# Where the modulated input and three heads' value weights begin in SBUF, in a pooling and mLSTM layer

## The chip, the cores and the metric

One core of a Trainium2 chip runs the kernel, in one launch. The metric is the device time of one execution in microseconds (us); lower is better. Three runs of the kernel before gave 889.26, 889.43 and 889.63 us, so the median is 889.43 us.

## The reference

One layer of a latent-token backbone: 512 latent tokens and 256 context tokens, 1024 channels, everything in fp32. Cut to what matters here:

```
a_lat = rmsnorm(x)   * norm_mix * (1 + sc1)  + sh1        # 512 x 1024, the modulated input
a_ctx = rmsnorm(ctx) * norm_mix * (1 + csc1) + csh1       # 256 x 1024
p     = a @ w_in      # pooled input, q, k, v, o, two branch gates, 16 mLSTM gate columns
h     = bidirectional mLSTM(q, k, v, gates), 4 heads of 256, chunks of 128
y     = sigmoid(p[5]) * pool_mixer(p[0]) + sigmoid(p[6]) * readout(h, p[4])
x     = x + g1 * (y @ w_out)
x     = x + g2 * (silu(b @ w_g) * (b @ w_u)) @ w_ffn_out,   b = modulated rmsnorm(x)
out   = rmsnorm(x) * norm_final
```

Only the latent tokens are an output. The context tokens need keys, values and gates, but no queries.

## The kernel before, in words

**Layout.** Activations lie transposed: channels on the 128 partitions, tokens along the free axis. The modulated input is eight tiles of 128 channels by 512 latent tokens, and the context's eight tiles of 256 tokens two to a buffer. Precision comes from splitting: every fp32 operand x is held as a high part (x rounded to the type fp32r) and a low part (x minus the high part), and a product is three matmuls, high by high, high by low and low by high. So the latent modulated input takes 16 buffers of the tag `a`, and the context's 8: 24 buffers of 128 x 512 values, 2048 bytes on each partition.

**The stages, in order.** (1) `mod_rows`, `mod_cols` and `stage` (lines 261 to 329) make scale and shift, the tiles of `a` (`modulate`, line 284: ACT writes the high part, DVE the low) and six first output tiles at once (`products`, line 331, matmuls on line 334). (2) `values(0)`, then for each of the four heads gates, queries, keys, values, `attention` and the pooling branch. A tile of 128 output columns of `a @ w_in` is made by `lat_tile` (line 403): `wload` (line 148) brings 128 x 1024 weights by DMA into a raw buffer, ACT rounds them into a `wh` buffer and DVE subtracts into a `wl` buffer, and `mm3` (line 180) does 24 matmuls with the weights as the stationary operand, which is loaded into TensorE, and a tile of `a` as the moving operand, which streams through it. `keys` (line 421) does the same for the 256 context tokens as well. (3) the output projection (`proj_out`), (4) the feed-forward network, whose input products are Strassen products (`front` and `back`) over tiles of the tag `hp`, and its second product (`ffn_out`) over tiles of the tag `act`.

**The order of the work.** Stage 1 and a part of stage 4 are written out by hand for PE, ACT and DVE; elsewhere a planner orders the instructions. The `wh` and `wl` buffers are two each, `wr` (raw) three.

**`values(h)`** (line 549) turns the roles round: a 128 x 128 block of `a` is stationary, the value weights of a head are moving, 256 columns of them (272 for head 0, with the 16 gate columns). For each of six token blocks it does 24 matmuls (lines 565 to 567).

**Where tiles begin.** Only the position of a tile's first byte on its partition, counted from a multiple of 256 bytes, is at issue here, so the list says where each matmul operand begins:

```
LINE = 256
NEXT = 48
def S(tag, dtype=F32):
    return tl(tag, [P, T], dtype, BUFS[tag], LINE)
wh, wl = (tl(t, [P, WMAX], F32R, 2, LINE)[:, skip:skip + n] for t in ("wh", "wl"))
_, wh, wl = wload(src[:, i * 4 * n:(i + 1) * 4 * n], 4 * n, skip=min(NEXT, WMAX - 4 * n))
tl("q", [P, T + NEXT], F32R, BUFS["q"], LINE)[:, NEXT:]
hp = [tl("hp", [P, NEXT + 7 * D + 4], F32R, 2, LINE) for _ in range(2)]
```

`S` puts every tile on a multiple of 256 bytes: `a`, `act`, `kq`, `Sp`, `oh`, `ol`. The weights of `wload` lie on one too, unless `skip` moves them. The queries and the Strassen operands `hp` begin 48 values, 192 bytes, behind a multiple (one of the seven parts of `hp`, T3, 208 bytes behind). The value weights of heads 1, 2 and 3 begin 192 bytes behind; those of head 0 are 1088 values to a half and fill the buffer, so `skip` is 0, and their four slices of 272 columns begin 0, 64, 128 and 192 bytes behind. Slices of 128 or 256 columns are 512 or 1024 bytes and keep the position of their tile.

Of the kernel before, what the change touches and what calls it, by code (L numbers as in the profile page):

```python
# [10 lines left out]
F32 = mybir.dt.float32  # L11
# [6 lines left out]
P = 128  # L18
D = 1024
KT = D // P  # L20
T = 512
# [9 lines left out]

BUFS = {"a": 24, "tmp": 7, "kq": 7, "q": 4, "E": 6, "Sp": 10, "m": 7, "pm": 4, "act": 16, "x1": 8, "oh": 5, "ol": 5}
LINE = 256
NEXT = 48
WMAX = KT // 2 * (DH + NG)
PBW = 15 * 71
# [13 lines left out]
def layer_kernel(ctx: ExitStack, tc, xT, cT, w0, w1, wv0, wv, wada_a, wada_b, par, crow, bg, wpool,  # L50
# [3 lines left out]
    cnt = [0]  # L54
    pools, homes, stacks = {}, {}, {}

    def open_pool(name, tags, side="left"):
        st = ExitStack()
        p = st.enter_context(tc.tile_pool(name=name, bufs=1, side=side, reuse_waits="tile"))
        pools[name] = p  # L60
        for t in tags:
            homes[t] = p
        stacks[name] = st
# [4 lines left out]
    def tl(tag, shape, dtype=F32, bufs=1, align=None):  # L68
        cnt[0] += 1
        return homes[tag].tile(shape, dtype, name=f"{tag}_{cnt[0]}", tag=tag, bufs=bufs, align_bytes=align)  # L70

    def S(tag, dtype=F32):
        return tl(tag, [P, T], dtype, BUFS[tag], LINE)

    ps = ctx.enter_context(tc.tile_pool(name="ps", bufs=4, space=PSUM))
    dram = ctx.enter_context(tc.tile_pool(name="dram", bufs=1, space=DRAM))
# [1 line left out]
    def PS(tag="ps"):  # L78
        cnt[0] += 1
        return ps.tile([P, 512], F32, name=f"{tag}{cnt[0]}", tag=tag, bufs=4)  # L80

    open_pool("main", ("wr", "wh", "wl", "tmp", "small", "rc", "rc2"))
    open_pool("ap", ("a",), "right")
    open_pool("mix", ("m", "pm", "pa", "pb"), "right")
    open_pool("kqp", ("kq", "q"))
    open_pool("st", ("x", "cx", "ada", "row"))
# [58 lines left out]
    def wide(tag, bufs=2):  # L145
        return tl(tag, [P, D], F32R, bufs, LINE)

    def wload(src, n, dst=None, skip=0):

        raw = tl("wr", [P, WMAX], F32, 3)  # L150
        nc.sync.dma_start(raw[:, :n], src)
        if dst is None:
            wh, wl = (tl(t, [P, WMAX], F32R, 2, LINE)[:, skip:skip + n] for t in ("wh", "wl"))
            nc.scalar.copy(wh, raw[:, :n])  # L154
            V.tensor_sub(wl, raw[:, :n], wh.bitcast(F32))  # L155
            return [(wh[:, i * P:(i + 1) * P], wl[:, i * P:(i + 1) * P]) for i in range(n // P)], wh, wl
        if dst == "wide":
            h, l = (wide(t)[:, skip:skip + n] for t in ("gh", "gl"))
            split(raw[:, :n], h, l)
            return [(h[:, i * P:(i + 1) * P], l[:, i * P:(i + 1) * P]) for i in range(n // P)], None, None  # L160
        if isinstance(dst, str):
            dst = (dst, dst)
        parts = []
        for c in range(0, n, T):
            m = min(T, n - c)
            h, l = (S(t, F32R) for t in dst)
            nc.scalar.copy(h[:, :m], raw[:, c:c + m])
            V.tensor_sub(l[:, :m], raw[:, c:c + m], h[:, :m].bitcast(F32))
            parts += [(h[:, i * P:(i + 1) * P], l[:, i * P:(i + 1) * P]) for i in range(m // P)]
        return parts, None, None  # L170

    def split(src, h, l):
        nc.scalar.copy(h, src)
        V.tensor_sub(l, src, h.bitcast(F32))
        return h, l

    def tsplit(src, tag):
        return split(src, S(tag, F32R), S(tag, F32R))
# [6 lines left out]
            nc.tensor.matmul(dst, wh, al, start=False, stop=False, skip_group_check=on)  # L185
            nc.tensor.matmul(dst, wl, ah, start=False, stop=last and i == n - 1, skip_group_check=on)  # L186

    def vload(src, n, i):

        _, wh, wl = wload(src[:, i * 4 * n:(i + 1) * 4 * n], 4 * n, skip=min(NEXT, WMAX - 4 * n))  # L190
        return [(wh[:, c * n:(c + 1) * n], wl[:, c * n:(c + 1) * n]) for c in range(4)]

    class SumSq:
# [90 lines left out]
    def modulate(src, r, scale, shift, h, l, between=None):  # L284
# [7 lines left out]
        V.scalar_tensor_tensor(l, t1, shift, h.bitcast(F32), ALU.add, ALU.subtract)  # L292
        return h, l

    aT, acT = [], []
    acc0 = [PS("ps" if i < 2 else "pat") for i in range(len(FIRST) - 1)] + [wbank]
    cxt = [tl("cx", [P, T], F32, 4) for _ in range(4)]
# [23 lines left out]
    def stage(k, r):  # L321

        n = len(FIRST) * P
        raw, wh, wl = tl("wr", [P, WMAX], F32, 3), tl("wh", [P, WMAX], F32R, 2, LINE), tl("wl", [P, WMAX], F32R, 2, LINE)
        nc.sync.dma_start(raw[:, :n], w0[k])
# [40 lines left out]
    for k in range(KT):  # L366
# [18 lines left out]
        if k in (5, 6):  # L385
            ctx_quad(4 * (k - 5))
    manual.__exit__(None, None, None)
    wv_first += vload(wv0, DH + NG, 1)
    acc0 = dict(zip(FIRST, acc0))


    def conv_part(acc, n, j, dsts=None):

        y = S("tmp")
        nc.scalar.activation(y[:, :n], acc[:, :n], AF.Identity, bias=pcol(C_CB, j), scale=pcol(C_CW, 16 + j))
        V.scalar_tensor_tensor(y[:, 1:n], acc[:, 0:n - 1], pcol(C_CW, j), y[:, 1:n], ALU.mult, ALU.add)
        V.scalar_tensor_tensor(y[:, 0:n - 1], acc[:, 1:n], pcol(C_CW, 32 + j), y[:, 0:n - 1], ALU.mult, ALU.add)
        s = S("tmp")
        tanh_half(s[:, :n], y[:, :n])
        gated(y[:, :n], s[:, :n], y[:, :n])  # L400
        return split(y[:, :n], *dsts) if dsts else tsplit(y, "kq")

    def lat_tile(idx):

        if idx in acc0:
            return acc0[idx]
        acc = PS()
        mm3(acc, wload(w1[idx], D)[0], aT)
        return acc
# [7 lines left out]
    def queries(h):  # L417
        return [conv_part(lat_tile(Q0 + 2 * h + dk), T, 2 * h + dk,
                          [tl("q", [P, T + NEXT], F32R, BUFS["q"], LINE)[:, NEXT:] for _ in range(2)]) for dk in range(2)]

# [97 lines left out]
    def late_mod(n, behind):  # L518

        for i in itertools.islice(late, n):  # L520
            wa = tl("pb", [P, PBW], F32, 2)
            nc.sync.dma_start(wa[:, :D], wada_b[i])
            with tc.issue_after(behind.ins):
                V.scalar_tensor_tensor(wa[:, :D], wa[:, :D], 0.5, crow_s, ALU.mult, ALU.mult,
                                       accum_out=mods[:, i:i + 1])
# [12 lines left out]
    def atok(i):  # L538

        src = acT if i < 2 else aT  # L540
        i -= 0 if i < 2 else 2
        return [(h[:, i * P:(i + 1) * P], l[:, i * P:(i + 1) * P]) for h, l in src]
# [6 lines left out]
    def values(h, wp=None):  # L549
        n = DH + NG if h == 0 else DH  # L550
        if wp is None:
            wp = vload(wv[h - 1], n, 0) + vload(wv[h - 1], n, 1)
        vh = tl("vh", [P, NTOK, DH + 2], F32R)
        vl = tl("vl", [P, NTOK, DH + 2], F32R)
        nc.gpsimd.memset(vh[:, :, DH:DH + 1].bitcast(F32), 1.0)
        nc.gpsimd.memset(vh[:, :, DH + 1:DH + 2].bitcast(F32), 0.0)
        nc.gpsimd.memset(vl[:, :, DH:DH + 2].bitcast(F32), 0.0)
        accs = {}
        for i, half in ((2, 0), (3, 0), (4, 0), (2, 1), (3, 1), (4, 1), (5, 0), (5, 1), (0, 0), (0, 1), (1, 0), (1, 1)):
            if half == 0:  # L560
                accs[i] = PS()
            acc = accs[i]
            for kk in range(4 * half, 4 * half + 4):
                (wh, wl), (ah, al) = wp[kk], atok(i)[kk]
                nc.tensor.matmul(acc[:, :n], ah, wh, start=kk == 0, stop=False)  # L565
                nc.tensor.matmul(acc[:, :n], ah, wl, start=False, stop=False)  # L566
                nc.tensor.matmul(acc[:, :n], al, wh, start=False, stop=kk == KT - 1)  # L567
            if half == 0:
                continue
            if h == 0:  # L570
                gsrc = acc[:, DH:DH + NG].rearrange("p (d c h) -> p d c h", d=2, c=2)
                bsrc = bgt.rearrange("p (d c h) -> p d c h", d=2, c=2)
                for d, j in ((0, i), (1, 1 - i if i < 2 else 7 - i)):
                    V.tensor_add(gif[:, :, d, j, :], gsrc[:, d], bsrc[:, d])
            nc.scalar.copy(vh[:, i, :DH], acc[:, :DH])
            low = V.tensor_sub(vl[:, i, :DH], acc[:, :DH], vh[:, i, :DH].bitcast(F32))
            if h:
                late_mod(1, low)
        return vh, vl
# [266 lines left out]
    for h in range(H):  # L846
        tg = None
        if h == 0:
            mgate_all(0)
            mgate_all(1)  # L850
            q_ = queries(0)
        v = values(h, None if h else wv_first)
        if h == 0:
            gen = gates()
# [85 lines left out]

    hp = [tl("hp", [P, NEXT + 7 * D + 4], F32R, 2, LINE) for _ in range(2)]
    B11, B21, B22, N1, N2, T4, T3 = ([t[:, o:o + D] for t in hp] for o in [NEXT + i * D + i // 6 * 4 for i in range(7)])
    B12 = None
# [431 lines left out]
```

## Time and profile before

| | |
|---|---|
| median of three runs | 889.43 us |
| profiled execution, first to last instruction | 888.3 us |
| TensorE matmuls (PE): busy, share, count | 877.0 us, 99%, 5920 |
| TensorE weight loads (PEld) | 799.2 us, 90%, 5920 |
| VectorE (DVE) | 613.7 us, 69% |
| ScalarE (ACT) | 434.9 us, 49% |
| DMA | 120.87 MB, mean 136 GB/s |
| granted TensorE clock | 0.999 of full speed |

The profiled execution's own time outside its span is not listed; its span stands 1.1 us under the median of the runs. A group of instructions is one line of code, one engine and one kind of operand, named out<-in: `ps<-a,wh` is a matmul that writes a PSUM tile from a tile of `a` and one of `wh`. A matmul's duration in the profile is its latency, not its share of the engine: matmuls overlap in the pipeline, so what one costs is the distance from its start to the next one's start, called the pitch below. It is read from two rows of the timeline and the number of matmuls between them.

### The profile page before, as it was taken

What the parts mean: (1) busy time and instruction counts of PE and PEld (TensorE: products, weight loads), DVE (VectorE), ACT (ScalarE), POOL (GpSimd) and SP (SyncE); (2) the same over time, 40 slices, a digit from 0 to 9 for tenths busy, and PEclk for the clock granted to TensorE, in tenths of its full rate; (3) what the DMA queues carried; (4) which work ended last, traced back from release to release, by engine and by line L of the source; (5) the groups of instructions that cost most, each with busy time, mean ns of one, the idle gap of its engine ahead of it and who ended that gap; (6) DMA issues with size and microseconds to landing.
All of it is one profiled execution on the core that took longest, in us unless ns stands there. A gap on an engine that the chain in (4) does not pass through costs nothing.

```text
span 888.3 us, 15038 instructions
## 1 busy us (share of the span) xinstructions
PE 877.0 (99%) x5920; PEld 799.2 (90%) x5920; DVE 613.7 (69%) x1187; ACT 434.9 (49%) x823; POOL 66.5 (7%) x93
## 2 busy tenths in 40 slices
PE   9999999999999999999999999999999999999996
PEld 8689798899888998889988899999889998899996
DVE  5678676868876787667886767884386744877544
ACT  4464363545345453354545446763156632656541
POOL 0000010010000100001000000110011100111000
PEclk9999999999999999999999999999999999999999
DMA  9853021445252632525443920474356642765402
GB/s 351 323 201 102 28 69 61 166 130 155 89 184 73 201 112 80 175 87 162 136 141 109 317 87 15 129 195 115 90 159 155 161 111 86 193 148 139 116 1 95
DMA packets 41445, 120.87 MB, mean 136 GB/s; under 512 B 4480, under 2 KB 8864, under 8 KB 40352
## 3 DMA queue, kind: packets, MB, share of 16 engines
q1 hardware_dynamic: 35904, 109.96, 37.9%
q0 software_dynamic: 5472, 9.96, 6.8%
q8 instruction: 46, 0.75, 0.3%
q14 instruction: 23, 0.19, 0.1%
HBM read 116.22 MB, written 3.69 MB: 135 GB/s over the span
## 4 chain that ended last, share of the span: by engine, by line
PE 89%; DVE 5%; ACT 2%; DMA 1%; issue 1%; DVEq 0%; ACTq 0%; SPq 0%
PE ps L184 20%; PE ps L186 20%; PE ps L185 20%; PE pat L334 3%; PE ps L565 3%; PE ps L566 3%; PE ps L567 3%; PE pat L781 2%; PE pat L780 2%; PE pat L779 2%; PE pat L185 2%; PE pat L184 2%; PE pat L186 2%; DMA wr<-in_wffo 1%; PE ps L334 1%; PE pat L739 1%
## 5 line engine op out<-in xcount | busy, mean ns | idle before, releaser
L184 PE MATMUL ps<-a,wh 128*128 128x512 f32 (+1 forms) x368 | 138.9, 377 | 0.0
L185 PE MATMUL ps<-a,wh 128*128 128x512 f32 (+1 forms) x368 | 138.5, 376 | 0.0
L186 PE MATMUL ps<-a,wl 128*128 128x512 f32 (+1 forms) x368 | 138.3, 376 | 0.0
L154 ACT CAST wh<-wr 128x1024 fp32r<-128x1024 f32 (+3 forms) x78 | 78.8, 1010 | 116.4 <-PE ps L185 89.2
L155 DVE TENSOR_TENSOR wl<-wr,wh 128x1024 fp32r<-128x1024 f32 (+3 forms) x78 | 91.7, 1176 | 44.1 <-ACT wh L154 42.9
L186 PEld LDWEIGHTS ps<-a,wl 128*128 128x128 f32 x368 | 69.3, 188 | 12.6
L184 PEld LDWEIGHTS ps<-a,wh 128*128 128x128 f32 x368 | 69.3, 188 | 12.1
L185 PEld LDWEIGHTS ps<-a,wh 128*128 128x128 f32 x368 | 69.3, 188 | 11.9
L186 PE MATMUL ps<-act,wl 128*128 128x512 f32 (+1 forms) x224 | 77.9, 348 | 0.9 <-DVE wl L155 0.9
L184 PE MATMUL ps<-act,wh 128*128 128x512 f32 (+1 forms) x224 | 78.0, 348 | 0.6 <-DVE tmp L1077 0.6
L185 PE MATMUL ps<-act,wh 128*128 128x512 f32 (+1 forms) x224 | 77.7, 347 | 0.0
L565 PE MATMUL ps<-wh,a 128*128 128x256 f32 (+1 forms) x192 | 54.4, 283 | 0.0
L567 PE MATMUL ps<-wh,a 128*128 128x256 f32 (+1 forms) x192 | 54.4, 283 | 0.0
L566 PE MATMUL ps<-wl,a 128*128 128x256 f32 (+1 forms) x192 | 54.3, 283 | 0.0
L1014 POOL DMA_DIRECT2D ol<-in_wffi x38 | 33.4, 887 | 255.8 <-ACT ol L1013 90.0
L1223 DVE SCALAR_TENSOR_TENSOR x<-ps,lb,x 128x512 f32<-128x512 f32 (+1 forms) x32 | 19.6, 616 | 45.5 <-PE ps L186 45.5
L184 PE MATMUL ps<-hp,gh 128*128 128x256 f32 x176 | 50.0, 284 | 1.0 <-ACT pat L1052 1.0
L184 PE MATMUL ps<-hp,oh 128*128 128x256 f32 x176 | 48.9, 278 | 0.1
L185 PE MATMUL ps<-hp,gh 128*128 128x256 f32 x176 | 48.9, 278 | 0.0
L186 PE MATMUL ps<-hp,gl 128*128 128x256 f32 x176 | 48.9, 278 | 0.0
L185 PE MATMUL ps<-hp,oh 128*128 128x256 f32 x176 | 48.7, 277 | 0.0
L186 PE MATMUL ps<-hp,ol 128*128 128x256 f32 x176 | 48.6, 277 | 0.0
(323 smaller groups left out, 2527.9 us busy)
## 6 DMA issues: line engine op xcount, KB each, us to landing
wr<-in_w SPq DMA_DIRECT2D x42, 512.0 KB, 3.5
pb<-in_wada_b SPq DMA_DIRECT2D x32, 512.0 KB, 4.1
wr<-in_wffi SPq DMA_DIRECT2D x25, 512.0 KB, 4.2
ur<-in_wffi SPq DMA_DIRECT2D x19, 512.0 KB, 3.9
ol<-in_wffi POOLq DMA_DIRECT2D x38, 256.0 KB, 4.9
ada<-in_wada_a SPq DMA_DIRECT2D x8, 1024.0 KB, 10.2
wr<-in_wffo SPq DMA_DIRECT2D x16, 448.0 KB, 3.8
wr<-in_wout SPq DMA_DIRECT2D x8, 512.0 KB, 3.6
```

Source lines behind the costliest of these rows:

```text
L154: nc.scalar.copy(wh, raw[:, :n])
L155: V.tensor_sub(wl, raw[:, :n], wh.bitcast(F32))
L184: nc.tensor.matmul(dst, wh, ah, start=first and i == 0, stop=False, skip_group_check=on)
L185: nc.tensor.matmul(dst, wh, al, start=False, stop=False, skip_group_check=on)
L186: nc.tensor.matmul(dst, wl, ah, start=False, stop=last and i == n - 1, skip_group_check=on)
L334: nc.tensor.matmul(acc0[i], w_first[k][i][w], aT[k][x], start=k + w + x == 0, stop=k == KT - 1 and w == 1)
L565: nc.tensor.matmul(acc[:, :n], ah, wh, start=kk == 0, stop=False)
L566: nc.tensor.matmul(acc[:, :n], ah, wl, start=False, stop=False)
L567: nc.tensor.matmul(acc[:, :n], al, wh, start=False, stop=kk == KT - 1)
L779: nc.tensor.matmul(o, sh_, vh[:, s, :], start=n == 0, stop=False)
L1014: nc.gpsimd.dma_start(l, dram, accum_op=ALU.add)
L1223: V.scalar_tensor_tensor(x1[j][:, c], acc[:, c], g2[:, j:j + 1], x1[j][:, c], ALU.mult, ALU.add)
```

## The change

The buffers of the tag `a` are asked for at multiples of 64 bytes, and a spacer of 48 values per partition is put into the same pool, so that all 24 buffers begin 192 bytes behind a multiple of 256. The value weights of heads 1 and 3 lose their offset and begin on a multiple; those of head 2 keep it, and head 0 is as it was. No instruction is added or removed, and none changes its shape.

```
+HALFLINE = 64
...
+    shifted = ("a",)
...
     def S(tag, dtype=F32):
-        return tl(tag, [P, T], dtype, BUFS[tag], LINE)
+        return tl(tag, [P, T], dtype, BUFS[tag], HALFLINE if tag in shifted else LINE)
...
-    open_pool("ap", ("a",), "right")
+    open_pool("ap", ("a", "behind_a"), "right")
...
-    def vload(src, n, i):
+    def vload(src, n, i, skip=NEXT):
-        _, wh, wl = wload(src[:, i * 4 * n:(i + 1) * 4 * n], 4 * n, skip=min(NEXT, WMAX - 4 * n))
+        _, wh, wl = wload(src[:, i * 4 * n:(i + 1) * 4 * n], 4 * n, skip=min(skip, WMAX - 4 * n))
...
+    tl("behind_a", [P, NEXT], F32, 1, HALFLINE)
     aT, acT = [], []
...
         if wp is None:
-            wp = vload(wv[h - 1], n, 0) + vload(wv[h - 1], n, 1)
+            skip = NEXT if h == 2 else 0
+            wp = vload(wv[h - 1], n, 0, skip) + vload(wv[h - 1], n, 1, skip)
```

## The prediction, made before the result was known

> **What bounds the kernel now.** I read the page first, then the waits of PE, then the groups by shape, then single starts in the timeline.
>
> ```profile
> span 888.3 us, 15038 instructions
> PE 877.0 (99%) x5920; PEld 799.2 (90%) x5920; DVE 613.7 (69%) x1187; ACT 434.9 (49%) x823; POOL 66.5 (7%) x93
> PE 89%; DVE 5%; ACT 2%; DMA 1%; issue 1%; DVEq 0%; ACTq 0%; SPq 0%
> ...
> ACT wh L154 <- PE ps L185: 89.2, 38, 5.2
> ```
>
> PE carries 89% of the chain that ended last, and it is busy nearly throughout. The last line says who is ahead: ACT, about to fill a `wh` buffer, waited 89.2 us in all for PE to give one back. The weights are ready before PE wants them, so time saved between two matmuls of these stages reaches the end of the kernel, and so does time lost. The change alters no instruction, so all that it can do is change the pitch of matmuls (the distance between two starts) that read `a`. Those are these groups:
>
> ```profile
> L184 PE MATMUL ps<-a,wh 128*128 128x512 f32 x320 | 125.4, 392 | 0.0
> L185 PE MATMUL ps<-a,wh 128*128 128x512 f32 x320 | 124.9, 390 | 0.0
> L186 PE MATMUL ps<-a,wl 128*128 128x512 f32 x320 | 124.7, 390 | 0.0
> ...
> L184 PE MATMUL ps<-act,wh 128*128 128x512 f32 x136 | 52.9, 389 | 0.0
> ...
> L565 PE MATMUL ps<-wh,a 128*128 128x256 f32 x144 | 40.5, 281 | 0.0
> ...
> L334 PE MATMUL pat<-a,wh 128*128 128x512 f32 x64 | 20.8, 403 | 0.0
> ...
> L565 PE MATMUL ps<-wh,a 128*128 128x272 f32 x48 | 13.9, 290 | 0.0
> L186 PE MATMUL ps<-a,wl 128*128 128x256 f32 x48 | 13.6, 283 | 0.0
> ...
> L334 PE MATMUL pat<-a,wl 128*128 128x512 f32 x32 | 12.6, 392 | 0.0
> ...
> L334 PE MATMUL ps<-a,wh 128*128 128x512 f32 x32 | 10.8, 415 | 0.2 <-ACT a L289 0.2
> L334 PE MATMUL ps<-a,wl 128*128 128x512 f32 x16 | 6.3, 394 | 0.0
> L184 PE MATMUL ps<-a,Sp 128*128 128x512 f32 x16 | 6.2, 391 | 0.0
> ...
> L185 PE MATMUL ps<-a,Sp 128*128 128x256 f32 x16 | 4.5, 283 | 0.0
> ```
>
> Counts: moving 512 columns of `a`, 3 x 320 + 3 x 16 = 1008 in the projections and 64 + 32 + 32 + 16 = 144 in the first stage; moving 256 columns of the context, 3 x 48 + 3 x 16 = 192; stationary `a`, 3 x 144 = 432 for heads 1 to 3 (144 a head) and 144 of 272 columns for head 0.
>
> **Does the pitch depend on where operands begin?** These pairs of rows are the first and the last of unbroken runs, in the timeline of PE (start, duration, line).
>
> ```profile
> 167.51 0.28 PE L184 MATMUL ps<-a,wh 128*128 128x256 f32 x1
> ...
> 170.26 0.28 PE L186 MATMUL ps<-a,wl 128*128 128x256 f32 x1
> ...
> 701.52 0.28 PE L184 MATMUL pat<-hp,wh 128*128 128x256 f32 x1
> ...
> 706.73 0.28 PE L185 MATMUL ps<-hp,oh 128*128 128x256 f32 x1
> ...
> 217.28 0.28 PE L739 MATMUL pat<-q,kq 128*128 128x256 f32 x1
> ...
> 221.37 0.39 PE L184 MATMUL ps<-a,wh 128*128 128x512 f32 x1
> ...
> 201.15 0.28 PE L739 MATMUL pat<-q,kq 128*128 128x256 f32 x1
> ...
> 205.39 0.39 PE L184 MATMUL ps<-a,wh 128*128 128x512 f32 x1
> ...
> 184.19 0.28 PE L565 MATMUL ps<-wh,a 128*128 128x256 f32 x1
> ...
> 188.43 0.28 PE L565 MATMUL ps<-wh,a 128*128 128x256 f32 x1
> ```
>
> The shape is the same in all five, 256 moving columns, and the pitch is not. Context keys, both operands on a multiple of 256: 24 matmuls, 23 steps, 2.75 us / 23 = 119.6 ns. Strassen, moving 192 behind and stationary on a multiple: four products of twelve, the quoted row is the 47th, 5.21 / 46 = 113.3 ns. Queries by keys, the same positions: three products of twelve up to the next group, 4.09 / 36 = 113.6 ns at one place and 4.24 / 36 = 117.8 ns at another. Values, moving 192 behind and stationary on a multiple: 4.24 / 36 = 117.8 ns. So with equal positions the pitch is 119.6, and with 192 between them it is 113.3 or 117.8, and one and the same pair of tiles can show either: it also matters in what rhythm a run is entered.
>
> The Trainium skill speaks against any such effect: "TensorE: Matmul & The Clock Gate", step-by-step section, gives PE two independent read ports, so that loading the next weights takes nothing from the running matmul, and "SBUF — State Buffer", "Who interferes with whom", says that PE never waits on anyone. By that rule the time stays at 889.4 us; the trace disagrees at 256 columns (119.6 against 113.3 ns).
>
> **What it does at 512 columns** is the disputed term, since 512 columns have run at equal positions only:
>
> ```profile
> 259.08 0.39 PE L184 MATMUL ps<-a,wh 128*128 128x512 f32 x1
> ...
> 269.73 0.39 PE L186 MATMUL ps<-a,wl 128*128 128x512 f32 x1
> ...
> 142.52 0.39 PE L184 MATMUL ps<-a,wh 128*128 128x512 f32 x1
> ...
> 144.60 0.39 PE L184 MATMUL ps<-a,wh 128*128 128x512 f32 x1
> ```
>
> ```profile
> 10.86 0.88 PE ps L349 x8
> ```
>
> Two tiles, 48 matmuls: 10.65 / 47 = 226.6 ns. That is exactly 2 x 113.3, the pitch of the good runs at 256. The single row, from the chain, is of matmuls with only 2 moving columns: they still come 0.88 / 8 = 110 ns apart, so a load of 128 x 128 weights sets about 110 ns by itself. At 256 columns the load is therefore the pace or nearly so, and an extra delay shows at once; at 512 columns there is twice the time, and the same delay in the load hides. I take it that 226.6 ns is already the undisturbed pitch at 512, and set this term at 0. The other end: at equal positions 256 more columns cost 226.6 - 119.6 = 107.0 ns, which leaves a constant of 119.6 - 107.0 = 12.6 ns on each matmul, and a good run at 256 has only 113.3 - 107.0 = 6.3 ns. If that constant goes with the position and not with the load, 512 columns save the difference, 6.3 ns, too. Then it is worth 1152 x 6.3 = 7.3 us.
>
> **The terms of the sum.** Three views give the last prices: the chain (writes of the same instruction to tiles at both positions), the page's groups of ACT and DVE that make the weights, and the groups by shape for the Strassen matmuls.
>
> ```profile
> 541.78 0.40 ACT act L961
> ...
> 543.65 0.40 ACT hp L961
> ```
>
> ```profile
> L154 ACT CAST wh<-wr 128x1024 fp32r<-128x1024 f32 (+3 forms) x78 | 78.8, 1010 | 116.4 <-PE ps L185 89.2
> L155 DVE TENSOR_TENSOR wl<-wr,wh 128x1024 fp32r<-128x1024 f32 (+3 forms) x78 | 91.7, 1176 | 44.1 <-ACT wh L154 42.9
> ...
> L184 PE MATMUL ps<-hp,oh 128*128 128x256 f32 x176 | 48.9, 278 | 0.1
> ```
>
> - Steady runs at 512 columns: 0.
> - Entries into runs at 512: the pair from 142.52 to 144.60 is the start of a tile just behind another stage: nine steps take 2.08 us, 231 ns each. The mean durations show such excess in all: against 389 for `act`, 320 x 3 + 320 x 1 + 320 x 1 = 1.6 us in the projections, and 64 x 14 + 32 x 3 + 32 x 26 + 16 x 5 = 1.9 us on L334. Bounds: 0 to 3.5 us gained, or as much lost if entries get longer. Runs of `hp` settle quickly, but part of L334 is waiting for new tiles that a position can't touch. I take half of the first and a sixth of the second: -1.1 us.
> - Context keys: 192 matmuls from 119.6 to between 113.3 and 117.8: -1.2 to -0.3 us. The keys are queued between long runs like the Strassen products, so I take 113.3: -1.2 us.
> - Values of head 2: both operands now 192 behind, equal again: 144 x (119.6 - 117.8) = +0.3 us.
> - Values of heads 1 and 3: stationary 192 behind, moving on a multiple, the reverse of now. No run has it; bounds 288 x (113.3 - 117.8) = -1.3 and 288 x (119.6 - 117.8) = +0.5 us. Nearest is the present pitch, 117.8: 0.
> - Values of head 0: its four slices begin 0, 64, 128 and 192 behind, and their distance from `a` only changes places: 0, bounds -0.5 and +0.5 us.
> - Writing `a` 192 behind: one activation each to `act` (on a multiple) and `hp` (192 behind) takes the same, so 0. The spacer is 192 bytes on a partition and issues nothing; no queue and no wait is touched. What hides a faster PE's need for weights is ACT's 89.2 us of lead; without it each tile would wait for ACT's cast and DVE's subtraction, 1.0 + 1.2 us.
>
> Sum: -1.1 - 1.2 + 0.3 = -2.0 us. The profiled span would go from 888.3 to 886.3, and the median, which stands 1.1 above the span, from 889.43 to 887.4 us. A measurement of this kernel can tell about 0.2%, 1.8 us, from no change.
>
> **The rivals.**
> - Fixed tax: every matmul with equal positions pays 6.3 ns, whatever its length. -7.3 - 1.2 + 0.3 = -8.2 us, 881.2 us. For it: one constant fits both lengths. Against it: the load's own pace explains 256 without it. Chance 0.18.
> - Half the tax: the long runs fall into the rhythm of 117.8, not of 113.3: 119.6 - 117.8 = 1.8 ns on 1152 is -2.1, keys -0.3, head 2 +0.3, entries -1.0: -3.1 us, 886.3 us. Chance 0.12.
> - Slower: at 512 columns 226.6 is undisturbed because equal positions keep the two streams apart in time, and 192 brings the disturbed rhythm of the queries and values into the projections, 117.8 - 113.3 = 4.5 ns. 1008 x 4.5 = +4.5, keys -0.3, head 2 +0.3, heads 1 and 3 +0.5: +5.0 us, 894.4 us; with every other run disturbed, 892. It decides as soon as the projections lose 1.1 + 1.2 - 0.3 = 2.0 us, 2.0 ns each. For it: the values show that 192 alone does not bring 113.3, and the slow entry at 231 ns shows that a run at 512 can be disturbed. Against: `hp` with `oh`, 176 matmuls a group, has a mean duration of 278 ns, that of the run at 113.3, where values have 281. Chance 0.18.
> - Nothing: either the pitch follows the rhythm alone and not the positions, or `a` is not put where the text says (a spacer that falls on the other side of the buffers would leave them on a multiple): 889.4 us. Against it stand 119.6 and 113.3, for it the two rhythms of one pair of tiles. Chance 0.10. The skill's rule above gives this time too.
>
> **How the numbers follow.** The forecast, 887.4 us, has 0.42; its own range is 885.0 (entries at their bound of -3.5, the rest as taken) to 889.4 (entries at 0 and keys at -0.3). Six tenths of it lie beyond 0.2% faster. Faster: 0.25 + 0.18 + 0.12 = 0.55. Same: 0.17 + 0.10 = 0.27. Slower: 0.18. The range for 8 in 10 reaches down to the fixed tax, 881.0, and up to the half-disturbed case, 892.0.
>
> **What would show it.** In the profile after: the context keys (256 columns of `a`) at 113 to 114 ns by starts, duration 277 or 278 instead of 283; the projections at 512 columns still at 226.6 in the middle of a run, and their mean durations near 389 instead of 392; values of head 2 at 119 to 120; values of heads 1 and 3 near 118. The forecast is wrong if a middle stretch of 48 matmuls at 512 columns takes 10.3 us (the tax) or 10.8 and more (the disturbed rhythm), or if the keys stay at 119.6.

## The result and the profile after

The changed kernel takes 894.94 us (median of five runs, 894.26 to 896.72) against 889.26 us for the kernel before on the same chip (888.55 to 889.63): a ratio of 1.0063, 95% interval 1.0053 to 1.0074. By that interval it is slower by 4.7 to 6.6 us, where 887.4 us was forecast. These are the lines of the page that answer to those of before, and the wait of ACT for a `wh` buffer (lines moved down by three behind the first edits):

```profile
span 893.2 us, 15038 instructions
PE 881.7 (99%) x5920; PEld 797.4 (89%) x5920; DVE 614.5 (69%) x1187; ACT 435.3 (49%) x823; POOL 66.0 (7%) x93
PE 90%; DVE 4%; ACT 2%; issue 2%; DMA 1%; DVEq 0%; POOLq 0%; POOL 0%; SPq 0%; ACTq 0%
...
L157 ACT CAST wh<-wr 128x1024 fp32r<-128x1024 f32 (+3 forms) x78 | 78.8, 1011 | 121.5 <-PE ps L188 93.8
```

The span grew by 4.9 us and PE's busy time by 4.7. DVE and ACT are as they were, and ACT waits a little longer for PE than before (93.8 against 89.2 us), so the weights are no later: the time is lost between matmuls. The groups by shape say where:

```profile
L187 PE MATMUL ps<-a,wh 128*128 128x512 f32 x320 | 126.9, 397 | 0.0
L188 PE MATMUL ps<-a,wh 128*128 128x512 f32 x320 | 126.5, 395 | 0.0
L189 PE MATMUL ps<-a,wl 128*128 128x512 f32 x320 | 126.4, 395 | 0.0
...
L338 PE MATMUL pat<-a,wh 128*128 128x512 f32 x64 | 20.9, 405 | 0.0
...
L187 PE MATMUL ps<-a,wh 128*128 128x256 f32 x48 | 13.3, 277 | 0.0
L188 PE MATMUL ps<-a,wh 128*128 128x256 f32 x48 | 13.3, 277 | 0.0
L189 PE MATMUL ps<-a,wl 128*128 128x256 f32 x48 | 13.3, 277 | 0.0
```

The durations of the 960 projection matmuls of 512 columns rose from 375.0 to 379.8 us in all; those of the 144 context keys fell from 40.8 to 39.9. Durations are latencies, so the pitch is read from starts again, in the timeline of PE. Each pair of rows is the first of a run and the first behind it, or, for the pair from 143.53, the first and the tenth of one run:

```profile
143.53 0.39 PE L187 MATMUL ps<-a,wh 128*128 128x512 f32 x1
...
145.63 0.39 PE L187 MATMUL ps<-a,wh 128*128 128x512 f32 x1
...
169.14 0.28 PE L187 MATMUL ps<-a,wh 128*128 128x256 f32 x1
...
171.97 0.39 PE L187 MATMUL ps<-a,wh 128*128 128x512 f32 x1
...
177.57 0.28 PE L187 MATMUL ps<-a,wh 128*128 128x256 f32 x1
...
180.30 0.39 PE L187 MATMUL ps<-a,wh 128*128 128x512 f32 x1
...
185.89 0.28 PE L570 MATMUL ps<-wh,a 128*128 128x256 f32 x1
...
202.85 0.28 PE L744 MATMUL pat<-q,kq 128*128 128x256 f32 x1
...
261.70 0.39 PE L187 MATMUL ps<-a,wh 128*128 128x512 f32 x1
...
272.90 0.28 PE L187 MATMUL ps<-a,wh 128*128 128x256 f32 x1
...
289.55 0.28 PE L570 MATMUL ps<-wh,a 128*128 128x256 f32 x1
...
306.80 0.28 PE L744 MATMUL pat<-q,kq 128*128 128x256 f32 x1
```

- 512 columns: 48 matmuls in 11.20 us, 233.3 ns; the same stretch took 226.6 before. A run goes at this pitch from its first steps (2.10 us / 9 = 233 ns).
- Context keys: 24 in 2.73 us, 113.8 ns, behind a run of 512 columns of `a`; but 24 in 2.83 us, 117.9 ns, at 169.14, behind a run of `pm`, whose operands both lie on a multiple. The positions are the same, and there are two pitches.
- Values of head 1: 144 in 16.96 us, 117.8 ns, as before. Values of head 2: 144 in 17.25 us, 119.8 ns.

The sum goes by starts too, each matmul at the distance to the next one's start, over the whole of both traces. The 1008 projection matmuls of 512 columns (the 960 and the 48 on `Sp`) went from 230.69 to 236.44 us, +5.75 or 5.7 ns each; the 144 of the first stage +0.37; the 192 context keys from 22.98 to 21.92, -1.06; head 2 +0.29. That is +5.35 us. All other matmuls together took 0.48 less, which leaves +4.87 of the span's +4.9 us.

### The profile page after: what moved, and what is told of

It reads as the page before. It is cut to its first block, busy times and chain, and to the rows that moved or that the text cites. A ratio compares the mean times of both kernels' runs of the same rounds, so it can differ in the third digit from the quotient of the medians.

```text
span 893.2 us, 15038 instructions
## 1 busy us (share of the span) xinstructions
PE 881.7 (99%) x5920; PEld 797.4 (89%) x5920; DVE 614.5 (69%) x1187; ACT 435.3 (49%) x823; POOL 66.0 (7%) x93
## 4 chain that ended last, share of the span: by engine, by line
PE 90%; DVE 4%; ACT 2%; issue 2%; DMA 1%; DVEq 0%; POOLq 0%; POOL 0%; SPq 0%; ACTq 0%
PE ps L187 20%; PE ps L189 20%; PE ps L188 20%; PE pat L338 3%; PE ps L572 3%; PE ps L571 3%; PE ps L570 3%; PE pat L786 2%; PE pat L784 2%; PE pat L785 2%; PE pat L189 2%; PE pat L187 2%; PE pat L188 2%; PE ps L338 1%; PE pat L745 1%
## 5 line engine op out<-in xcount | busy, mean ns | idle before, releaser
L157 ACT CAST wh<-wr 128x1024 fp32r<-128x1024 f32 (+3 forms) x78 | 78.8, 1011 | 121.5 <-PE ps L188 93.8
```

## The experiments

Theory 1: at 512 columns the distance, modulo 256 bytes, between the first bytes of the moving and the stationary operand sets the pitch; 0 is best. At 256 columns it offers two pitches, and the run ahead decides which (theory 1a, formed on the way, when the context keys showed two). Theory 2: the moving operand alone must lie on a multiple of 256. Theory 3: the spacer and the place of the pool, or the value weights, cost the time. Rival 1b to 1a: at 256 columns too, the pair of positions alone decides. "At 192, 0" below means moving 192 bytes behind a multiple and stationary on one.

**Positions tried one by one.** The kernel before, with runs of 30 matmuls on tiles of `hp` added behind its end, for all pairs of interest. They compute nothing of the result.

```
+    def trial(n, mo, so, wide=P):
+        for i in range(30):
+            j, e = divmod(i, 3)
+            m = hp[0][:, 64 + mo // 4 + 2560 * (e == 1) + 256 * j:][:, :n]
+            s = hp[1][:, 64 + so // 4 + 2560 * (e == 2) + 128 * j:][:, :wide]
+            nc.tensor.matmul(banks[3][:wide, :n], s, m, start=True, stop=True)
...
```

> The kernel before with 69 short runs of 30 extra matmuls each behind its end, all on the Strassen operands and with results that nobody reads, so its total time says nothing; what counts is the pitch in each run. The moving operand has 512 or 256 columns and begins 0 to 240 bytes behind a multiple of 256, the stationary one on a multiple (and the reverse, and equal positions other than 0), and four runs load only 32 columns of weights instead of 128. Theory 1 (the distance between the two positions sets the pitch): 512 columns at 0 and 0 give 226.7 ns, at 192 and 0 233.3, at 192 and 192 and at 64 and 64 226.7 again; 256 columns at 0 and 0 give 120, at 192 and 0 113.3 or 117.8, at 192 and 192 120. Theory 2 (the moving position alone): 512 columns give 233.3 at 192 and 192 as well, and 226.7 with the stationary one moved. On what the floor is: if 226.7 is the undisturbed pitch at 512 columns, loading only 32 columns leaves it at 226.7 and takes 192 and 0 back to it; if the load disturbs both, both fall below 226.7, to 214 to 220.

Each row of the timeline below is a part of one run: its start, the time from the first start to the last end, and the number of matmuls. Less the last one's own latency (0.39 us at 512 columns, 0.28 at 256, as in rows above), divided by the steps, it gives the pitch.

```profile
883.25 4.47 PE L1291 MATMUL ps<-hp,hp 128*128 128x512 f32 x19
...
904.26 4.51 PE L1291 MATMUL ps<-hp,hp 128*128 128x512 f32 x19
...
931.75 4.83 PE L1291 MATMUL ps<-hp,hp 128*128 128x512 f32 x20
...
958.79 2.44 PE L1291 MATMUL ps<-hp,hp 128*128 128x256 f32 x19
...
969.73 1.98 PE L1291 MATMUL ps<-hp,hp 128*128 128x256 f32 x16
...
1064.63 4.97 PE L1291 MATMUL ps<-hp,hp 128*128 128x512 f32 x21
...
1082.82 4.02 PE L1291 MATMUL ps<-hp,hp 128*128 128x512 f32 x17
...
1098.24 5.03 PE L1291 MATMUL ps<-hp,hp 128*32 128x512 f32 x21
```

In this order: 512 columns at 0, 0: 4.08 / 18 = 226.7 ns; at 64, 0: 228.9; at 192, 0: 4.44 / 19 = 233.7; 256 columns at 0, 0: 120.0; at 64, 0: 113.3; 512 at 0, 192 (a distance of 64): 229.0; at 192, 192: 226.9; and at 0, 0 with only 32 weight columns to load: 232. By the starts of the last 18 steps, 512 columns at 16, 32, 96, 128, 160, 208 and 224, 0 took 232 to 235 ns, and at 240, 0 once 226.7 and once 236.6; 256 columns at all positions but 0, 64 and 192 took 116.4 to 120.0. Nothing at 512 columns ran under 226.6, and equal positions gave that pitch wherever they lay (64, 64 too, 226.7). Theory 1 holds here at 512 columns, but for 240; theory 2 falls.

The four runs with 32 weight columns came out as neither of the two ways expected. 512 columns took 231.6 ns at 0, 0 and 231.7 at 192, 0, and 256 columns 113.3 at both. A shorter load does not help equal positions at 512, and with it the position no longer made a difference, so the load of the weights has a part in the effect. Whether 226.6 is an undisturbed pitch these runs don't show; it is the lowest found.

**Weights at 192 as well.** The kernel after, with the weights of the projections and of the first stage moved too, so that `a` and its weights are equal again. Only head 0's key weights stay on a multiple: they lie in tiles of `Sp`, and that branch of `wload` uses no offset.

```
+        wh, wl = wh[:, NEXT:], wl[:, NEXT:]
...
-        mm3(acc, wload(w1[idx], D)[0], aT)
+        mm3(acc, wload(w1[idx], D, None, NEXT)[0], aT)
...
-            w = wload(w1[K0 + 2 * h + dk], D, None if h else "Sp")[0]
+            w = wload(w1[K0 + 2 * h + dk], D, None if h else "Sp", NEXT)[0]
```

> The changed kernel with the weights of the projections, of the keys and of the first stage also 192 bytes behind a multiple, as the modulated input is, so that positions are equal again. Theory 1 (distance): projections back from 233.3 to 226.7 ns in the middle of a run, context keys back from 114 to 119.6, values as in the changed kernel; 894.9 - 1152 x 4.6 ns + 192 x 5.6 ns = 890.7 us, between 889.5 and 891. Theory 2 (the moving position alone): projections stay at 233.3 and keys at 114, 894 to 896 us.

889.51 us, ratio to before 1.0005 (0.9995 to 1.0015): the loss is gone with `a` still 192 behind. Its timeline, the same two tiles:

```profile
258.68 0.39 PE L187 MATMUL ps<-a,wh 128*128 128x512 f32 x1
...
269.58 0.28 PE L187 MATMUL ps<-a,wh 128*128 128x256 f32 x1
```

10.90 us / 48 = 227.1 ns. Head 0's keys are a control in the same kernel: by starts their 48 matmuls of 512 columns still took 233.1 ns each, as in the kernel after, against 227.8 in the kernel before. Theory 2 is refuted in the kernel itself, and so is a part of theory 3: spacer and pool are those of the kernel after.

**Only the context moved.** The kernel before, with the eight context buffers under a tag of their own at 192.

```
...
-                tt, hh, ll = S("tmp"), S("a", F32R), S("a", F32R)
+                tt, hh, ll = S("tmp"), S("ac", F32R), S("ac", F32R)
```

> The kernel before with only the context's 8 buffers 192 bytes behind a multiple; the latent 16 stay on one, all value weights as before. Both theories: projections at 226.7 ns in the middle of a run, context keys from 119.6 to 113.3 to 114.5, 192 x 5.6 = -1.1 us; values of the two context blocks of heads 1 to 3 get equal positions, 144 x 2.0 = +0.3 us; sum -0.8 us, 888.5 us. If the slower time of the changed kernel came from anything else than the latent tiles at 512 columns (the spacer, the pool's place), this kernel would be slower than before too, by up to 5 us.

889.33 us, ratio 0.9996 (0.9987 to 1.0005), no measurable change, where 888.5 was expected. The second key tile of head 1 in the timeline:

```profile
175.97 0.28 PE L187 MATMUL ps<-ac,wh 128*128 128x256 f32 x1
...
178.80 0.39 PE L187 MATMUL ps<-a,wh 128*128 128x512 f32 x1
```

2.83 us / 24 = 117.9 ns, and all six key tiles of heads 1 to 3 are alike (of head 0's two, one took 117.8 and one, right behind values, 114.2). So this tile did not reach the 113.8 that the same positions gave at the same place in the kernel after (177.57). What differs is the run ahead: 512 columns at equal positions here, at 192, 0 there. That is where theory 1a comes from.

**The input at 64 instead of 192**, and **the second part of the change undone**, both on the kernel after.

```
-    tl("behind_a", [P, NEXT], F32, 1, HALFLINE)
...
+        if k == 0:
+            tl("behind_a", [P, 32], F32, 1, HALFLINE)
```

> The kernel after with its 24 buffers of the modulated input 64 bytes behind a multiple of 256 instead of 192 (all else as after: value weights of heads 1 and 3 on a multiple, of head 2 at 192). Theory 1 (the distance between the two operands decides, as the trials priced it): 512 columns at 64 against weights on a multiple run at 228.9 ns, against a mean of 227.7 in the kernel before: 1152 x 1.2 = +1.4 us; context keys between 113.3 and 117.9 against 119.6: -1.2 to -0.3; head 2 at a distance of 128, 118.9 against 117.8: +0.2; so 889.8 to 890.7 us, no measurable change against before. Rival (whatever takes the input off the multiple costs the same): 233.3 ns and 894 to 895 us, as after.

```
-            skip = NEXT if h == 2 else 0
+            skip = NEXT
```

> The kernel after with the second part of the change undone: value weights of heads 1 and 3 at 192 again, so in all of heads 1 to 3 both operands lie 192 behind. Theory 1: equal positions, 119.9 ns against 117.8 in after on 288 matmuls: +0.6 us on after, 895.5 us; the slowdown is all in the 512-column matmuls. Rival (the value weights on a multiple against a at 192 are a part of the slowdown): 894.3 us or less.

At 64: 890.29 us, ratio 1.001 (1.0001 to 1.0019), as theory 1 had it, and not the 894 of the rival. Values at 192 again: 895.84 us, ratio 1.0073 (1.0059 to 1.0086), near the 895.5 of theory 1 and not under the kernel after: the value weights are no part of the loss, and theory 3 is gone. The timeline of the kernel at 64 holds something more:

```profile
184.50 0.28 PE L571 MATMUL ps<-wh,a 128*128 128x256 f32 x1
...
200.85 0.28 PE L745 MATMUL pat<-q,kq 128*128 128x256 f32 x1
...
259.09 0.40 PE L187 MATMUL ps<-a,wh 128*128 128x512 f32 x1
...
270.09 0.28 PE L187 MATMUL ps<-a,wh 128*128 128x256 f32 x1
```

512 columns go at 11.00 / 48 = 229.2 ns, but head 1's values at 16.35 / 144 = 113.5 ns, a pitch that they have in neither kernel of the change.

**The best single positions put together.** The kernel before with value weights at 64 and the Strassen part T3 at 192, the better places of the first trials.

```
...
-skip=min(NEXT, WMAX - 4 * n))
+skip=min(16, WMAX - 4 * n))
...
-[NEXT + i * D + i // 6 * 4 for i in range(7)]
+[NEXT + i * D for i in range(7)]
```

> The kernel before with two sets of 256-column matmuls moved to the best distances of the trials, and the 512-column ones left alone: value weights of heads 1 to 3 at 64 instead of 192 (432 matmuls), and the Strassen part T3 at 192 instead of 208 (about 228 matmuls). Theory 1 with the trials' prices: values 117.8 to 113.3, 432 x 4.5 = -1.9 us; T3 118.9 to 114.1, 228 x 4.8 = -1.1 us; 886.3 us. Rival (at 256 columns the rhythm in which a run is entered decides, not the distance alone): values stay at 117.8, T3 alone gains, 888.2 us.

891.72 us, ratio 1.0026 (1.0016 to 1.0036): slower, which neither had. In its timeline, head 1's values and the stretch of Strassen products that the prediction quotes:

```profile
184.45 0.28 PE L565 MATMUL ps<-wh,a 128*128 128x256 f32 x1
...
201.41 0.28 PE L739 MATMUL pat<-q,kq 128*128 128x256 f32 x1
...
702.67 0.28 PE L184 MATMUL pat<-hp,wh 128*128 128x256 f32 x1
...
708.09 0.28 PE L185 MATMUL ps<-hp,oh 128*128 128x256 f32 x1
```

The values stay at 117.8 ns. And the Strassen stretch, 46 steps on tiles whose positions were not touched, goes from 5.21 to 5.42 us, 113.3 to 117.8 ns: over all of `hp`, the mean pitch at 192 rose by starts from 116.7 to 118.6 ns on 1584 matmuls, +3.1 us, against 0.5 us saved on T3. Up to the first of T3 the Strassen products of both kernels go at the same pitches. One of the next T3 runs shows what it does. First the kernel before, then this one:

```profile
584.70 0.28 PE L184 MATMUL ps<-hp,gh 128*128 128x256 f32 x1
...
586.12 0.28 PE L184 MATMUL ps<-hp,wh 128*128 128x256 f32 x1
...
588.94 0.28 PE L184 MATMUL pat<-hp,wh 128*128 128x256 f32 x1
...
591.66 0.28 PE L184 MATMUL ps<-hp,oh 128*128 128x256 f32 x1
```

```profile
584.96 0.28 PE L184 MATMUL ps<-hp,gh 128*128 128x256 f32 x1
...
586.37 0.28 PE L184 MATMUL ps<-hp,wh 128*128 128x256 f32 x1
...
589.20 0.28 PE L184 MATMUL pat<-hp,wh 128*128 128x256 f32 x1
...
592.03 0.28 PE L184 MATMUL ps<-hp,oh 128*128 128x256 f32 x1
```

Both come to T3 (the second row of each four) at 118 ns: 12 steps in 1.42 and 1.41 us. From the third row on, 24 steps take 2.72 us with T3 at 208, 113.3 ns, and 2.83 with T3 at 192, 117.9. So the runs of T3 at 208 had led the others into the fast rhythm. A pair's pitch, measured alone, is not a price that can be added.

**What the run ahead does.** More trials behind the end of the kernel before; first by length, then 256 columns behind two kinds of run.

```
...
+    main = [(n, mo, 0) for mo in (0, 64, 192) for n in range(224, 513, 32)]
+    more = [c for so in (64, 192) for c in ((512, 0, 0), (256, 0, so), (512, 192, 0), (256, 0, so))]
+    more += [c for mo in (64, 192) for c in ((512, 0, 0), (256, mo, 0), (512, 192, 0), (256, mo, 0))]
...
```

> The kernel before with 70 more runs of 30 matmuls behind its end; their total time means nothing, their pitches are read. First: moving tiles of 224 to 512 columns in steps of 32, beginning 0, 64 and 192 behind a multiple, weights on a multiple. If the position acts by the way in which the moving stream and the weight load come to lie against each other, the sign differs by length: at 320 and 384 no difference (146.7 and 173.3 ns at 0 and 192 before), at 256 and 448 a gain at 192, at 512 a loss, and the excess over columns / 2.4 GHz lies near 6.7, 13.3 or 20 ns. If instead a position costs or saves a constant, or something per column, 288, 352, 416 and 480 fall on a straight line between their neighbours. Second: runs of 256 columns entered behind a run of 512 with equal positions or behind one with 192 between them. If the entry decides the rhythm, 256 at 192 runs at 117.8 behind the first and at 113.3 behind the second; if the pair of positions decides, both show one pitch, 113.3 where the moving tile is moved and 117.8 where the weights are.

Pitch in ns by starts, mean of the last 18 steps of each run, weights on a multiple:

| columns | 224 | 256 | 288 | 320 | 352 | 384 | 416 | 448 | 480 | 512 |
|---|---|---|---|---|---|---|---|---|---|---|
| moving at 0 | 111.8 | 120.0 | 131.6 | 146.7 | 160.0 | 173.3 | 188.4 | 202.7 | 216.7 | 226.7 |
| at 64 | 111.4 | 117.8 | 132.2 | 146.7 | 160.0 | 173.3 | 188.1 | 200.0 | 218.3 | 228.9 |
| at 192 | 111.4 | 113.3 | 133.3 | 146.6 | 160.0 | 174.8 | 186.7 | 202.2 | 215.8 | 233.3 |

From 320 to 384 columns a column costs 26.7 / 64 = 0.417 ns. Over that, 512 columns pay 13.3 ns at 0 and 20.0 at 192, 256 columns 13.3 and 6.7, and 320 and 352 the same 13.3 at every position. The sign of the effect depends on the length, as the first theory of this run had it. Two of its details did not come: the gain at 448 is 0.5 ns, and what 288, 416 and 480 columns pay at 0 (11.6, 15.1 and 16.7 ns) is none of the sizes that it named. The second part, 256 columns at 192, 0 behind 512 columns at 0, 0 and then behind 512 at 192, 0:

```profile
1101.63 2.05 PE L1291 MATMUL ps<-hp,hp 128*128 128x256 f32 x16
...
1112.47 2.09 PE L1291 MATMUL ps<-hp,hp 128*128 128x256 f32 x17
```

1.77 / 15 = 118 ns and 1.81 / 16 = 113 ns: one pair of positions, two steady rhythms, set by the run ahead. At 0, 64 it was the same (117.8 and 113.3); at 64, 0 and at 0, 192 both were 117.8, so a run ahead does not always do it.

**Putting that to use.** The second key tile of a head is the run of 512 columns ahead of its values. Its weights moved by 64, then by 192, on the kernel before:

```
-            w = wload(w1[K0 + 2 * h + dk], D, None if h else "Sp")[0]
+            w = wload(w1[K0 + 2 * h + dk], D, None if h else "Sp", 16 * dk)[0]
```

> The kernel before with one kind of tile moved: the weights of the second key tile of heads 1 to 3 begin 64 behind a multiple instead of on one; the input stays on a multiple and the values' weights at 192. So the 24 matmuls of 512 columns right ahead of each head's values run disturbed. Theory 1a (a run of 256 columns takes one of two rhythms, 117.8 or 113.3, by the run ahead of it, and holds it): those 3 x 24 matmuls go from 226.7 to 233.3, +0.5 us, and the 432 matmuls of the values from 117.8 to 113.3, -1.9 us; with the context keys of these tiles 119.7 to 117.8, -0.1: 887.8 us. Rival 1b (the pair of positions alone sets the pitch): values stay at 117.8 and the kernel takes 889.7 us.

> The same with these key weights at 192 instead of 64, a distance at which 512 columns run at 228.9 ns. Theory 1a, if any disturbed run leads into the fast rhythm: +0.2 us on the 72 matmuls, -1.9 on the values, 887.5 us. If only the other distance does it, or by rival 1b, values stay at 117.8: 889.4 us.

889.49 us, ratio 1.0001 (0.9992 to 1.001), and 889.29 us, 0.9999 (0.999 to 1.0008). In both the values kept 117.8 ns (head 1's 144 in 16.96 us), as rival 1b had it. With them went trials of how many matmuls it takes, after 24 at equal positions:

```
...
+    for mo, so in ((192, 0), (0, 64), (0, 192), (64, 0), (128, 0)):
+        for count in (1, 3, 6, 24):
+            trial(512, 0, 0, 0, 24)
+            trial(512, mo, so, 24 - count, count)
+            trial(256, 192, 0)
```

> The kernel before with 20 groups of three runs behind its end (the total time means nothing): 24 matmuls of 512 columns at equal positions, then 1, 3, 6 or 24 of 512 columns at another pair of positions (moving and stationary at 192 and 0, 0 and 64, 0 and 192, 64 and 0, 128 and 0), then 30 of 256 columns at 192 and 0. Theory 1a: without enough of the middle run the last one goes at 117.8 ns, behind 24 of it at 192 and 0 at 113.3, and the count from which it changes can be read; rival 1b: one pitch in all 20.

Last runs of three of the 20 groups (256 columns at 192, 0), behind 24 matmuls at 192, 0, behind one at 0, 64, and behind 24 at 0, 64:

```profile
922.55 1.98 PE L1291 MATMUL ps<-hp,hp 128*128 128x256 f32 x16
...
931.66 1.98 PE L1291 MATMUL ps<-hp,hp 128*128 128x256 f32 x16
...
966.13 1.93 PE L1291 MATMUL ps<-hp,hp 128*128 128x256 f32 x15
```

1.70 / 15 = 113.3 ns twice, then 1.65 / 14 = 117.9. In all 20, each of which ran once: behind 192, 0 the fast rhythm for any count; behind 0, 64 for one and three, not for six and 24; behind 0, 192 for one alone; behind 128, 0 for six and 24; behind 64, 0 never. So rival 1b is refuted, and the two kernels before this had simply used the counts (24 at 0, 64 and at 0, 192) that lead to the slow rhythm. One matmul should do it:

```
...
+                V.tensor_sub(wl[:, :m], raw[:, :m], wh[:, :m].bitcast(F32))
+                V.tensor_sub(wl[:, kick + m:kick + n], raw[:, m:n], wh[:, m:n].bitcast(F32))
+                return [(wh[:, i:i + P], wl[:, i + kick * (i == m):][:, :P]) for i in range(0, n, P)], wh, wl
...
```

> The kernel before, with the low parts of the last 128 weight rows of the second key tile of heads 1 to 3 put 64 behind a multiple (one more DVE subtraction for each tile). So one matmul of 512 columns, the last ahead of each head's values, is off its equal position. In the trials one such matmul was followed by 256 columns at 113.3 ns, 24 of them by 117.8. Theory 1a: the values of heads 1 to 3 run at 113.3 instead of 117.8: 432 x 4.5 = -1.9 us, the scores behind them perhaps another -0.4 us, nothing else changes: 887.1 to 887.6 us. Rival 1b, and also a state that only the trials' way into it brings about: values stay at 117.8, 889.4 us.

888.12 us, ratio 0.9986 (0.9977 to 0.9995): faster than both kernels, with PE's instructions in the same order. Head 1's values:

```profile
184.59 0.28 PE L572 MATMUL ps<-wh,a 128*128 128x256 f32 x1
...
200.93 0.28 PE L746 MATMUL pat<-q,kq 128*128 128x256 f32 x1
```

16.34 / 144 = 113.5 ns, where the kernel before has 184.19 to 201.15, 117.8; heads 2 and 3 are alike. One matmul's weights, 64 bytes further on, speed up the 144 behind it. By starts the values of heads 1 to 3 fell from 50.9 to 49.0 us and the scores behind them from 33.2 to 32.8, as forecast. Of the whole time the forecast was 1.8 to 2.3 us gained; the median gained 1.3, and the interval (0.4 to 2.0 us) reaches no further than the low part of the forecast.

## Why the prediction was wrong, point by point

- **Steady runs at 512 columns, set at 0.** This is the step that failed: "at 512 columns there is twice the time, and the same delay in the load hides. I take it that 226.6 ns is already the undisturbed pitch at 512, and set this term at 0." That no position goes under 226.6 was right as far as tried. What does not follow is that moving `a` leaves it so: 226.6 is the pitch of equal positions, and 192 between them makes it 233.3. The time that 512 columns leave to the load does not hide the difference. The term was +5.75 us on the projections and +0.37 on the first stage. That the load sets the pace at 256 columns has support (32 weight columns bring equal positions from 120.0 to 113.3 ns there), but at 512 a quarter of the load gave 231.6 ns, not less than 226.6.
- **Entries, -1.1.** Over the steady pitch the 1008 projection matmuls carried 2.2 us before (230.7 against 1008 x 226.7 ns) and carry 1.3 after (236.4 against 1008 x 233.3 ns). So less is lost on entries, but there is hardly anything left to settle: runs now start at 233 ns, near the 231 of an entry before, and stay there. The group on L334, now L338, rose from 403 to 405 ns instead of falling. The fact on which the term stood, 231 ns in an entry before, was the sign that a run at 512 can be disturbed; it was priced as a loss to be won back, not as the state that the change would make permanent.
- **Context keys, -1.2.** The 192 gained 1.06 us, and seven of the eight tiles run at 113 to 114 ns as forecast. But the size is partly luck, since it goes with the disturbed run ahead: behind `pm`, and in seven of eight tiles where 512 columns stay undisturbed (the context moved alone), they run at 117.8 ns. So the largest gain that was forecast depended on the loss that was not.
- **Values.** Head 2 at 119.8 (forecast 119.6), heads 1 and 3 at 117.8: right. The reverse of the positions cost nothing; the trials at 0, 192 gave 117.8 too, behind either kind of run.
- **What hides a faster or slower PE.** ACT still waits for PE (93.8 us), and the matmuls that were not moved changed by 0.5 us in all: right.
- **The rivals.** The one that came true was "Slower", at 894.4 us: "192 brings the disturbed rhythm of the queries and values into the projections". That 192 brings a slower pitch to the projections is what the runs show; that equal positions help because they keep two streams apart in time is not shown. Its size was taken from 256 columns, 4.5 ns, where steady runs lost 6.7 and all 1008 together, with the entries counted, 5.7. That its 894.4 lies so near 894.94 is luck: it also had the keys gain 0.3 us, not 1.06, and heads 1 and 3 lose 0.5, not nothing. The fixed tax had a true half: a constant of about 13 ns over 0.417 a column is there at equal positions at 256, 320, 352, 384 and 512 columns alike (but not at 288, 416, 448 and 480, with 11.6 to 16.7). But the tax isn't lifted by moving: at 512 columns it grows. Two lengths that fit one constant were no ground for its sign at the third case, other positions at 512, which no row of the trace of before showed.
- **The Trainium skill's rule.** "SBUF — State Buffer" in the Trainium skill, "Who interferes with whom", says that PE never waits on anyone. The section is about one engine beside another. It is no guide to this effect: two kernels with the same instructions and the same input positions, the kernel after and that with weights at 192 too, differ by 233.3 against 227.1 ns a matmul and by 5.2 us (ratios to before of 1.0063 and 1.0005).

Left open: which part of the chip makes the distance matter (the runs show only that with 32 of 128 weight columns it no longer does), and why a given number of matmuls at a given distance ends in the one or the other rhythm. The runs give the table, not the cause.

## What to carry to other kernels

Where PE is the bound, look at the first byte of both operands of a matmul, modulo 256: in this kernel runs of 512 fp32r columns want them equal, and other distances cost 1 to 4% (226.7 against 228.9 to 236.6 ns; 240 bytes once cost nothing); runs of 256 columns do best 64 or 192 apart, and may then still go at either of two pitches, 113.3 or 117.8 ns. Before moving a buffer for the sake of one use, list the matmuls that read it by length and count: 192 matmuls were to gain 6 ns, and 1152 lost 5. A pitch that differs between two places of one and the same pair of tiles says that what ran ahead matters; try such a change in the kernel, not only by itself.

## What the runs showed of the hardware that was not expected

- At 512 columns the distance (moving less stationary, modulo 256) counts, not the position: 0, 0, 64, 64 and 192, 192 give 226.6 to 226.7 ns; 64, 0 and 0, 192, both a distance of 64, give 228.9; 192, 0 and 0, 64, both a distance of 192, give 233.3. At 128 the two sides differ a little, 232.5 and 233.3 against 231.9.
- With 32 weight columns in place of 128 the position made no difference: 231.6 and 231.7 ns at 512 columns, 113.3 twice at 256.
- Position has no effect at 320 and 352 columns (146.7 and 160.0 ns at 0, 64 and 192), and opposite effects at 256 and 512. Two pitches of one pair are not peculiar to 256 columns: 448 at 0, 0 took 206.7 ns in the first trials and 202.7 in the second, 512 at 240, 0 took 226.7 and 236.6.
- A rhythm outlives what set it: one matmul at another distance changed the pitch of the 144 behind it by 4.3 ns each, and 12 matmuls of T3 at 208 brought the products behind them, which do not read T3, from 118 to 113.3 ns, which the same 12 at 192 did not.
